# Second matmul of each attention score block: 64 rows of a head against 128 rows with zeros beside them

## The chip, the cores and the metric

The kernel runs on one core of one Trainium2 chip. The metric is the device time of one launch in microseconds (us); the number used is the median of the runs. A core has five engines with queues of their own: PE (TensorE, matmuls; PEld is its weight load, which can run beside a matmul), DVE (VectorE), ACT (ScalarE), POOL (GpSimd) and SP (SyncE, which here only issues transfers). Each engine takes its instructions in order and waits on semaphores for the others.

## What is computed

One decoder layer over 1024 prompt tokens and 32 sample tokens (8 sequences of 4): an mLSTM of 4 heads beside a dilated attention of 8 heads of 64, an output projection, a cross attention over a memory of 256, and a SwiGLU, all in float32. What the change touches is the attention over the prompt. The reference runs three dilated windows and weighs them by their softmax denominators:

```python
for window, d in DILATED:
    ...
    s = jnp.einsum('bdnqhe,bdnkhe->bdnhqk', qs, kb) * scale
    s = jnp.where(valid[None, :, None, :, :], s, -jnp.inf)
    p, lse = softmax_lse(s)
    ...
return combine_branches(outs, lses)
```

The kernel does the same as one causal softmax over all earlier keys, with the logarithm of how many windows hold a key added to its score (table LM). So each head needs, for each tile of 128 query tokens, the product of its q (64 channels) with its k (64 channels) over 128 to 1024 keys.

## The kernel before, in words

Float32 products run as fp32r, in parts: a value is split into a high part (rounded to fp32r) and a low part (the rest), and a product is made of high times high, high times low and low times high. In the big projections (`unit`, `tunit`) that is three matmuls of 128 rows for each slice of 128 channels.

The mixing layer goes over four pairs of heads (i = 0 to 3). For each: `project_qk(i)` makes q and k of the pair; `attention(i)` is a generator whose steps are traced as side work between the units of the projections that follow (`hook`): in pair 0 between the units of `project_m`, in pairs 1 to 3 between the token tiles of `project_v`. All matmuls are issued by one helper line, L276, and all transposes of the attention by L651.

`project_qk` lays a head's q out so that one matmul of 128 rows makes two of the three products: buffer `qz[hh]` holds the head's high part on one half of the partitions and its low part on the other half, `kz[hh]` holds the high part of k on both halves. The first matmul of a score block, `qz` times `kz`, is therefore (high + low) times high, over 128 rows. What is left is high times low: the low parts of k lie in `kl`, head 0 on partitions 0 to 63, head 1 on partitions 64 to 127, and the second matmul of the block takes the 64 partitions of its own head alone (`qz[hh][r, q]` times `kl[r, ks]`). Both add into the same PSUM bank.

A job is one query tile t (0 to 7) of one head hh; its 128(t+1) keys are done in one or two blocks (512 and the rest; 640 is 384 and 256). That is 12 blocks a head, 24 a pair, 96 in all. A step of the generator makes the scores of job j (PE), adds LM and takes the row maximum (DVE, L633), takes the exponential (ACT, L638), divides (DVE, L639 and L640); a few jobs later (`lag`: 2 in pairs 0 to 2, 1 in pair 3) `turn` transposes the probabilities (PE, L651) and copies them out of PSUM (L652, on ACT and DVE in turn), and `values` multiplies them with v into 64 columns each.

The order on PE, DVE, ACT and POOL is set by a scheduler from the traced order and its own cost estimates; the SP queue keeps the order in which it was written. Buffers are columns of a few big arenas: `f_all` and `f_x` for float32, `g_all` for high and low parts.

Of the kernel before, what the change touches and what calls it, by code (L numbers as in the profile page):

```python
# [31 lines left out]
# columns of the packed per-channel parameters  # L32
# [5 lines left out]
class Arena:  # L38
    """Columns of one memory location, taken and given back while the program is traced."""
# [41 lines left out]
class Zone:  # L81
    """Arenas that serve one kind of data."""
# [11 lines left out]
class Parts:  # L94
    """Tiles [P, n] as a high and a low part each, that the tensor engine multiplies at its full rate."""
# [39 lines left out]
def body(tc, ctx, I, O):  # L135
# [5 lines left out]
    # F: float32, G: high and low parts; NX and NY change over from one to the other.  # L141
# [9 lines left out]
    ar.arenas.append(arena(xpool.enter_context(tc.tile_pool(name="sbx", bufs=1)), NX + NY, "f_x"))  # L151
# [64 lines left out]
    # where the high and the low part of a slot are  # L216
# [3 lines left out]
    # the slot of a weight tile, and the tile whose readers have to be traced before it is loaded  # L220
# [28 lines left out]
    def weight():  # L249
        """The next weight tile: [P, 8, 128] as high and low parts."""  # L250
        j = W.at
        wload(j)
        W.at += 1
        return wtile(j)

    def weights(n):
        """The next n weight tiles, to be used together."""
        wload(W.at)
        out = [wtile(j) for j in range(W.at, W.at + n)]
        W.at += n  # L260
        assert W.at <= W.sent
        return out

    def weight_pair():
        """The next two weight tiles as one moving operand by k, [P, 2, 128], and their order."""
        wload(W.at)
        out = []
        for part in range(2):
            a, b = (wat[slot_of[j]][part] for j in (W.at, W.at + 1))
            lo, step = min(a, b), abs(a - b)  # L270
            out.append(R(gall[:, lo:lo + 2 * step]).rearrange("p (a x) -> p a x", a=2))
        W.at += 2
        return tuple((lambda k, v=v: v[:, :, P * k:P * k + P]) for v in out), a < b
# [6 lines left out]
    def later(units, fn):  # L280
        """Trace fn after that many more units of the tensor engine's work."""
        pending.append([units, fn])
# [15 lines left out]
    def hook(n=1):  # L298
        """Trace the next n pieces of the work that goes between units."""
        for _ in range(n):  # L300
            while sides:
                try:
                    next(sides[0])
                    break
                except StopIteration:
                    sides.pop(0)
# [5 lines left out]
    def unit(out, w, x, n0, n, K=KT):  # L312
        """out = sum over k of w[k].T x[k], from high and low parts."""
        s = slice(n0, n0 + n)
        for k in range(K):
            mm(out, w[0][:, k], x.rh(k, s), k == 0, False)
            mm(out, w[0][:, k], x.rl(k, s), False, False)
            mm(out, w[1][:, k], x.rh(k, s), False, k == K - 1)

    def tunit(out, x, n0, n, w, by_pass=False):  # L320
        """out = sum over k of x[k].T w[k]: tokens on partitions."""
        s = slice(n0, n0 + n)
        passes = [(x.rh, 0), (x.rh, 1), (x.rl, 0)]
        todo = [(k, p) for p in passes for k in range(KT)] if by_pass else [(k, p) for k in range(KT) for p in passes]
        for j, (k, (xp, a)) in enumerate(todo):
            mm(out, xp(k, s), w[a](k), j == 0, j == len(todo) - 1)

# [1 line left out]
    small = Ring([ar.take(12) for _ in range(12)])  # L329

    def newton(v, n):
        """v[:, :n] ** -0.5, by bits and three Newton steps."""
        h, y, a = small.next()[:, :n], small.next()[:, :n], small.next()[:, :n]
        vec.tensor_scalar(h, v, -0.5, None, ALU.mult)
        vec.tensor_scalar(y.bitcast(I32), v.bitcast(I32), -0.5, float(0x5F3759DF), ALU.mult, ALU.add)
        for _ in range(3):
            if n > 3:
                vec.tensor_tensor(a, y, y, ALU.mult)
                vec.tensor_tensor(a, a, h, ALU.mult)
                vec.scalar_tensor_tensor(y, a, 1.5, y, ALU.add, ALU.mult)  # L340
                continue
            c = [slice(j, j + 1) for j in range(n)]
            for j in c:
                vec.scalar_tensor_tensor(a[:, j], y[:, j], h[:, j], y[:, j], ALU.mult, ALU.mult)  # L344
            for j in c:
                vec.scalar_tensor_tensor(y[:, j], a[:, j], 1.5, y[:, j], ALU.add, ALU.mult)  # L346
        return y

    def rstd(sqs, n, rcol, rbc):
        """From squares [P, n], to be added up: 1/rms by token as columns, and over all partitions; two steps to trace."""  # L350
# [29 lines left out]
    ones = ar.take(P)  # L380
    vec.memset(ones.ap, 1.0)

# [10 lines left out]
    # buffers of the attention, and of the mLSTM; x, the sample's attention and the memory have them for a while  # L393
# [17 lines left out]
    def squares(raw, n):  # L411
        """The squares' sums over k, in place."""
# [54 lines left out]
    # buffers of an iteration  # L467
# [3 lines left out]
    # a head's q: high and low parts on a half of the partitions each; its k: high parts on both, low parts as q's high  # L471
    qz, kz = ([qkz[:, NP * (2 * a + hh):NP * (2 * a + hh) + NP] for hh in range(2)] for a in range(2))
    kl = qkz[:, 4 * NP:5 * NP]
    tmp = Ring([take(384) for _ in range(4)])
# [18 lines left out]
    # gates  # L493
    ig_tm = take(64)
    gr = take(2 * 160).view(k=2, t=160)
# [5 lines left out]
    def gates():  # L501
        ga = Arena(bcbuf.ap, bcbuf.n)
        ge = [ga.take(160) for _ in range(4)]
        pb = mb()
# [22 lines left out]
        # prompt: rows (chunk, head)  # L527
# [5 lines left out]
        vec.tensor_tensor_scan(b_, ones[:32, 0:128], lf[:, 0:128], 0.0, op0=ALU.mult, op1=ALU.add)  # L533
# [29 lines left out]
        # sample: rows head, columns (t, b)  # L563
# [27 lines left out]
        # to tokens on partitions, and over all partitions  # L591
# [11 lines left out]
        mm(p2[:, 192:224], ones[:32, :], wcd[:32, :], True, True)  # L603
# [9 lines left out]
    def attention(i):  # L613
        # the third buffer and the fourth are the mLSTM's, but the sample's attention has these in the last iteration
# [4 lines left out]
        sxs, pts = {}, {}  # L619

        def scores(j):
            t, hh = jobs[j]
            cn = P * (t + 1)
            r, q = slice(64 * hh, 64 * hh + 64), slice(P * t, P * t + P)
            sx = sxs[j] = SX.next()
            last = None
            for o, w in ((0, 384), (384, 256)) if cn == 640 else [(o, min(512, cn - o)) for o in range(0, cn, 512)]:
# [3 lines left out]
                mm(pb[:, :w], R(qz[hh][r, q]), R(kl[r, ks]), False, True)  # L631
# [31 lines left out]

        for j in range(15 + vlag):
            if j < 16:
                scores(j)
            if 0 <= j - lag < 16:
# [6 lines left out]
    def conv(j, n0, n, ps, dst):  # L674
        """Block n0..n0+n of tile j of the conv: its raw projection is ps times rstd."""
# [27 lines left out]
    def mlstm(h):  # L703
# [5 lines left out]
        # exp(u_s - mu_t), causal  # L709
# [23 lines left out]
        # the states between chunks, in place of what they come from  # L733
# [23 lines left out]
        # sample  # L757
# [30 lines left out]
        # divide, LayerNorm, gate  # L788
# [282 lines left out]
    qkz.drop()  # L1071
    for b in phase:
# [12 lines left out]
    def residual(xin, src, spill, xout, g, blocks):  # L1085
        """x = xin @ w + src, spilled; its parts times g, and the sums of its squares."""
# [36 lines left out]
    def xkv(j):  # L1123
        """A half of the memory's K or V."""
# [17 lines left out]
    def xscores(hp, t):  # L1142
        """The probabilities of two heads for 128 tokens."""
# [46 lines left out]
    def xsample():  # L1190
        """The sample's attention over the memory's caches, in pieces to trace between the others' work."""
# [68 lines left out]
    def xgroup(hp, n0, n):  # L1260
        """A pair of heads for a block, in pieces to trace between units."""
# [139 lines left out]
def layouts(x):  # L1401
    """The program's inputs: the arrays in the program's order of dimensions, and tables of shapes."""
# [4 lines left out]
    def chan(a):  # L1407
        """[n, 1024] to [128, 8, n]."""
        return c(a.T.reshape(8, P, -1).transpose(1, 0, 2))

    def wt(w):
        """[1024, N] to tiles [N / 128, 128, 8, 128]."""
# [30 lines left out]
    # tables  # L1443
# [21 lines left out]
def unpack(o):  # L1465
    """The reference's outputs from the program's."""
# [3 lines left out]
    def tok(a):  # L1470
        """[128, k, n] to [n, k * 128]."""
# [36 lines left out]
```

## Time and profile before

| | us |
|---|---|
| time, median of 3 runs (1815.0 to 1819.98) | 1817.07 |
| profiled execution: span from the first to the last instruction | 1815.7 |
| PE busy in that span | 1778.4 (98%) |
| PEld busy | 1678.2 (92%) |
| DVE busy | 989.5 (54%) |
| ACT busy | 568.0 (31%) |
| POOL busy | 256.8 (14%) |

The profile names the span alone as the profiled execution's own time. A PE that is shown busy is not a PE at its peak: a matmul's shown duration reaches from its start to its modelled end, and the next one starts before that end. What a matmul costs in a stream is the distance from its start to the next start. PEld's rows show the same from the other side: the time that the weight load stood idle before an instruction.

### The profile page before, as it was taken

The page shows a single profiled execution, that of the slowest core. Times are in us where ns is not written, and L with a number is a line of the kernel's source. Part 1 is how long each engine was busy: PE and PEld are TensorE (multiplying, and loading weights), DVE is VectorE, ACT ScalarE, POOL GpSimd, SP SyncE. Part 2 cuts the span into 40 slices and gives each one's busy share as a digit, 9 for nine tenths or more (in the row PEclk, how much of TensorE's full clock was granted, in tenths as well). Part 3 has the DMA queues.
Part 4 walks back from the last instruction along what each step waited for, and adds up shares of the span by engine and source line. Part 5 has one row for each costly group of instructions (what it writes and reads, how often), then busy time and mean ns, then how long its engine had stood idle before and what let it go on. Part 6 is the DMA issues. An engine that isn't in the chain of part 4 may idle for free.

```text
span 1815.7 us, 29027 instructions
## 1 busy us (share of the span) xinstructions
PE 1778.4 (98%) x11720; PEld 1678.2 (92%) x11720; DVE 989.5 (54%) x2418; ACT 568.0 (31%) x1132; POOL 256.8 (14%) x318
## 2 busy tenths in 40 slices
PE   6999999999999999999999999999999999999996
PEld 6879889889867899989989999999999999999996
DVE  7877676677646754666554535334433433444346
ACT  5344343343324453344343222211111120211214
POOL 3200200100100313200014211100101010010114
PEclk9999999999999999999999999999999999999998
DMA  4202112112233664475444511111111110111102
GB/s 164 67 31 74 56 53 73 52 55 71 96 111 135 205 217 142 143 254 199 151 148 141 192 51 47 48 36 58 47 35 47 47 59 24 59 47 47 47 13 96
DMA packets 60648, 165.09 MB, mean 91 GB/s; under 512 B 7234, under 2 KB 27618, under 8 KB 59874
## 3 DMA queue, kind: packets, MB, share of 16 engines
q1 hardware_dynamic: 52834, 139.79, 23.2%
q0 software_dynamic: 7680, 23.45, 3.6%
q8 instruction: 92, 1.51, 0.4%
q14 instruction: 42, 0.34, 0.1%
HBM read 135.41 MB, written 27.80 MB: 90 GB/s over the span
## 4 chain that ended last, share of the span: by engine, by line
PE 91%; DVE 5%; DMA 2%; ACT 1%; issue 1%; POOL 0%; DVEq 0%; SPq 0%; ACTq 0%; POOLq 0%
PE banks L276 88%; PE banks L651 2%; DVE g_all L409 1%; DVE g_all L235 1%; DVE f_all L1375 1%; DMA f_all<-in_w_mq_dram 1%; DMA f_x<-rowsD 1%; ACT g_all L234 0%; DVE f_x L693 0%; PE banks L1170 0%; DVE f_all L346 0%; DMA f_all<-in_xT_dram 0%; PE banks L818 0%; DMA f_all<-in_w_mk_dram 0%; DVE f_all L344 0%
## 5 line engine op out<-in xcount | busy, mean ns | idle before, releaser
L276 PE MATMUL banks<-g_all 128*128 128x384 f32 (+5 forms) x7104 | 1210.0, 321 | 12.7 <-DVE g_all L427 9.5
L276 PEld LDWEIGHTS banks<-g_all 128*128 128x128 f32 (+1 forms) x7104 | 1104.3, 189 | 63.5 <-issue 40.5
L276 PE MATMUL banks<-g_x,g_all 128*128 128x384 f32 (+3 forms) x1272 | 250.0, 325 | 0.0
L234 ACT CAST g_all<-f_all 128x1024 fp32r<-128x1024 f32 x136 | 141.6, 1047 | 277.2 <-PE banks L276 227.3
L276 PEld LDWEIGHTS banks<-g_x,g_all 128*128 128x128 f32 x1272 | 212.9, 189 | 0.7 <-issue 0.4
L235 DVE TENSOR_TENSOR g_all<-f_all,g_all 128x1024 fp32r<-128x1024 f32 x136 | 173.7, 1281 | 57.8 <-ACT g_all L234 57.4
L1355 DVE SCALAR_TENSOR_TENSOR f_all<-banks,f_all 128x384 f32<-128x384 f32 (+3 forms) x192 | 98.8, 522 | 133.1 <-PE banks L276 132.7
L1337 POOL TENSOR_TENSOR f_y<-f_y 128x384 f32<-128x384 f32 (+1 forms) x66 | 62.3, 943 | 637.8 <-DVE f_y L1336 637.8
L276 PE MATMUL banks<-g_all,g_x 128*128 128x384 f32 (+1 forms) x864 | 148.4, 323 | 0.0
L276 PEld LDWEIGHTS banks<-g_all,g_x 128*128 128x128 f32 x864 | 140.6, 188 | 0.0
L1336 DVE TENSOR_TENSOR f_y<-banks,f_all 128x384 f32<-128x384 f32 (+1 forms) x66 | 34.6, 524 | 109.2 <-PE banks L276 109.2
L276 PE MATMUL banks<-f_x 128*128 128x129 f32 (+6 forms) x542 | 84.7, 312 | 1.3 <-DVE f_x L724 0.9
L276 PEld LDWEIGHTS banks<-f_x 128*128 128x128 f32 (+3 forms) x542 | 60.8, 166 | 14.1 <-issue 4.7
L1333 DVE TENSOR_TENSOR f_y<-banks,f_all 128x384 f32<-128x384 f32 (+1 forms) x66 | 34.6, 524 | 68.7 <-PE banks L276 67.4
L1334 ACT ACTIVATE f_y<-f_y 128x384 f32<-128x384 f32 (+1 forms) x66 | 32.8, 497 | 124.4 <-DVE f_y L1333 124.4
L1095 DVE TENSOR_TENSOR f_all<-banks,f_all 128x384 f32<-128x384 f32 (+1 forms) x48 | 25.1, 522 | 73.8 <-PE banks L276 73.8
L276 PE MATMUL banks<-g_x 128*128 128x384 f32 (+3 forms) x288 | 63.1, 327 | 0.0
L1339 ACT CAST g_x<-f_y 128x384 fp32r<-128x384 f32 (+1 forms) x36 | 17.5, 487 | 117.5 <-POOL f_y L1337 117.5
L1335 DVE SCALAR_TENSOR_TENSOR f_y<-f_y 128x384 f32<-128x384 f32 (+1 forms) x66 | 34.5, 523 | 28.5 <-ACT f_y L1334 28.5
L276 PE MATMUL banks<-f_all,f_x 128*64 128x128 f32 (+4 forms) x558 | 48.8, 276 | 0.9 <-DVE f_x L537 0.9
L276 PEld LDWEIGHTS banks<-g_x 128*128 128x128 f32 x288 | 49.3, 191 | 0.1
L276 PEld LDWEIGHTS banks<-f_all,f_x 128*64 128x64 f32 (+4 forms) x558 | 37.4, 133 | 12.4 <-issue 7.2
(326 smaller groups left out, 1552.0 us busy)
## 6 DMA issues: line engine op xcount, KB each, us to landing
f_all<-in_w_mq_dram SPq DMA_DIRECT2D x24, 512.0 KB, 4.5
f_all<-in_w_gate_dram SPq DMA_DIRECT2D x22, 512.0 KB, 3.3
f_all<-in_w_up_dram SPq DMA_DIRECT2D x22, 512.0 KB, 3.3
f_all<-in_w_down_dram SPq DMA_DIRECT2D x22, 512.0 KB, 3.3
f_all<-in_w_cm_dram SPq DMA_DIRECT2D x20, 512.0 KB, 3.6
f_all<-in_memK_dram SPq DMA_DIRECT2D x16, 512.0 KB, 5.9
f_all<-in_memV_dram SPq DMA_DIRECT2D x16, 512.0 KB, 3.5
f_all<-x3T SPq DMA_DIRECT2D x4, 1056.0 KB, 4.9
```

Source lines behind the costliest of these rows:

```text
L234: act.copy(R(dst_hi), raw)
L235: eng.tensor_tensor(R(dst_lo), raw, dst_hi, ALU.subtract)
L276: pe.matmul(out, l, r, start=start, stop=stop)
L409: vec.scalar_tensor_tensor(x.rl(k, o), raw[:, k], col(g + k), x.hi(k, o), ALU.mult, ALU.subtract)
L651: pe.transpose(pb[:, c:c + P], sx[:, o + c:o + c + P], ident.ap)
L1095: vec.tensor_tensor(x, pb[:, :n], t, ALU.add)
L1333: vec.tensor_tensor(z, pg[:, :n], rbc[:, n0:n0 + n], ALU.mult)
L1334: act.activation(th, z, AF.Tanh, scale=0.5)
L1335: vec.scalar_tensor_tensor(z, th, 1.0, z, ALU.add, ALU.mult)
L1336: vec.tensor_tensor(bu, pu[:, :n], rbc[:, n0:n0 + n], ALU.mult)
L1337: gp.tensor_tensor(z, z, bu, ALU.mult)
L1355: vec.scalar_tensor_tensor(x, pb[:, :n], 0.5, x, ALU.mult, ALU.add)
```

## The change

The second matmul of a score block gets a stationary operand of 128 rows: the head's high part of q on its own 64 partitions, zeros on the other 64. It multiplies the low parts of k of both heads (`kl` on all 128 partitions); the zeros take the other head's away. The high part is copied by ACT into one of two buffers of 128 columns for each head (`pad`), two jobs ahead; a buffer comes up again four jobs later. The zeros are written once, at the start, by DVE. Room for the four buffers comes from a new small arena (`g_p`, 384 columns, taken from the end of `f_x`) and 128 columns of `g_all`; to make up for it a tile of ones is dropped (`one[:, 0:1]`, broadcast, stands for it) and the gates' staging tile `gr` moves into a buffer that the mLSTM uses later. The rest of the diff takes comments out.

```diff
-    ar.arenas.append(arena(xpool.enter_context(tc.tile_pool(name="sbx", bufs=1)), NX + NY, "f_x"))
+    ar.arenas.append(arena(xpool.enter_context(tc.tile_pool(name="sbx", bufs=1)), NX + NY - 3 * P, "f_x"))
+    padz = arena(xpool.enter_context(tc.tile_pool(name="sbq", bufs=1)), 3 * P, "g_p")
...
-    ones = ar.take(P)
-    vec.memset(ones.ap, 1.0)
...
+    qpad = [Ring([padz.take(P), padz.take(P) or gz.take(P)]) for _ in range(2)]
+    for ring in qpad:
+        for b in ring.items:
+            vec.tensor_scalar(R(b.ap), ident.ap, 0.0, None, ALU.mult)
...
-    gr = take(2 * 160).view(k=2, t=160)
...
+        gr = ga.take(2 * 160).view(k=2, t=160)
...
+        def pad(j):
+            t, hh = jobs[j]
+            r = slice(64 * hh, 64 * hh + 64)
+            qps[j] = qpad[hh].next()
+            act.copy(R(qps[j][r]), qz[hh][r, P * t:P * t + P])
...
-            r, q = slice(64 * hh, 64 * hh + 64), slice(P * t, P * t + P)
+            q, qp_ = slice(P * t, P * t + P), qps.pop(j)
...
-                mm(pb[:, :w], R(qz[hh][r, q]), R(kl[r, ks]), False, True)
+                mm(pb[:, :w], R(qp_.ap), R(kl[:, ks]), False, True)
...
+        pad(0), pad(1)
         for j in range(15 + vlag):
             if j < 16:
                 scores(j)
+            if j < 14:
+                pad(j + 2)
```

On PE the order stays. This is pair 1, query tiles 2 and 3, before; a row gives the shape that is written, so the second matmul of a block reads like the first (the "x2" of 384 and of 512 columns are one block each):

```order
179 L276 MATMUL banks<-g_all 128x384 x2
180 L651 MATMUL banks<-f_all,f_x 128x128 x2
181 L276 MATMUL banks<-g_all 128x384 x2
182 L651 MATMUL banks<-f_all 128x128 x2
183 L276 MATMUL banks<-f_all,f_x 64x128 x2
184 L276 MATMUL banks<-g_all 128x256 x24
185 L276 MATMUL banks<-g_all 128x512 x2
186 L651 MATMUL banks<-f_all 128x128 x3
```

The same place of the changed kernel (L660 is the transpose, L277 the helper, `g_p` the new buffers):

```order
207 L277 MATMUL banks<-g_all 128x384
208 L277 MATMUL banks<-g_all,g_p 128x384
209 L660 MATMUL banks<-f_all,f_x 128x128 x2
210 L277 MATMUL banks<-g_all 128x384
211 L277 MATMUL banks<-g_all,g_p 128x384
212 L660 MATMUL banks<-f_all 128x128 x2
213 L277 MATMUL banks<-f_all,f_x 64x128 x2
214 L277 MATMUL banks<-g_all 128x256 x24
215 L277 MATMUL banks<-g_all 128x512
216 L277 MATMUL banks<-g_all,g_p 128x512
217 L660 MATMUL banks<-f_all 128x128 x3
```

Every matmul stands where it stood; only the second of each block has another stationary operand.

On ACT there are 64 new copies. This is the start of pair 1's attention before (L865 takes v out of PSUM, L638 is the exponential, L652 the copy of transposed probabilities):

```order
114 L865 ACTIVATE f_x<-banks,f_all 128x128 x2
115 L638 ACTIVATE f_all,f_x<-f_all,f_x 128x128 x2
116 L865 ACTIVATE f_x<-banks,f_all 128x128
117 L652 COPY f_all<-banks 128x128
118 L638 ACTIVATE f_x<-f_x 128x256
119 L638 ACTIVATE f_all,f_x<-f_all,f_x 128x256
120 L865 ACTIVATE f_x<-banks,f_all 128x128
```

And of the changed kernel (L628 is the new copy, L877, L647 and L661 are what L865, L638 and L652 were):

```order
128 L877 ACTIVATE f_x<-banks,f_all 128x128 x2
129 L628 CAST g_p<-g_all 64x128 x2
130 L647 ACTIVATE f_all,f_x<-f_all,f_x 128x128 x2
131 L877 ACTIVATE f_x<-banks,f_all 128x128
132 L628 CAST g_p<-g_all 64x128
133 L628 CAST g_all<-g_all 64x128
134 L661 COPY f_all<-banks 128x128
135 L647 ACTIVATE f_x,f_all<-f_x,f_all 128x256
136 L647 ACTIVATE f_all<-f_all 128x256
137 L877 ACTIVATE f_x<-banks,f_all 128x128
```

The copies for jobs 0 to 3 stand further ahead, among the casts of `project_qk`; those shown are for jobs 4 to 7, each pair of them ahead of the exponentials or of the copy that stood there.

On DVE, at the start, before (L427 and L428 are the parts of the first v weights, L409 the low parts of x):

```order
8 L427 CAST g_all<-f_all 128x1056
9 L409 SCALAR_TENSOR_TENSOR g_all<-f_all,g_all 128x128
10 L428 TENSOR_TENSOR g_all<-f_all,g_all 128x1056
11 L427 CAST g_all<-f_all 128x1056
12 L409 SCALAR_TENSOR_TENSOR g_all<-f_all,g_all 128x128
13 L428 TENSOR_TENSOR g_all<-f_all,g_all 128x1056
14 L409 SCALAR_TENSOR_TENSOR g_all<-f_all,g_all 128x128
```

And of the changed kernel (L476 writes the zeros; L425, L426 and L407 are what L427, L428 and L409 were):

```order
9 L425 CAST g_all<-f_all 128x1056
10 L476 TENSOR_SCALAR g_p<-f_all 128x128
11 L426 TENSOR_TENSOR g_all<-f_all,g_all 128x1056
12 L476 TENSOR_SCALAR g_p<-f_all 128x128 x2
13 L476 TENSOR_SCALAR g_all<-f_all 128x128
14 L407 SCALAR_TENSOR_TENSOR g_all<-f_all,g_all 128x128 x2
15 L407 SCALAR_TENSOR_TENSOR g_all<-f_x,f_all,g_all 128x256 x8
```

Four new instructions stand ahead of the last low parts of the first chunk of x and of all of the second chunk's. The SP queue is unchanged.

## Rows read from the trace of the kernel before

**Rows 1.** The page: busy time, granted clock in 40 slices, chain by engine.

```profile
PE 1778.4 (98%) x11720; PEld 1678.2 (92%) x11720; DVE 989.5 (54%) x2418; ACT 568.0 (31%) x1132; POOL 256.8 (14%) x318
...
PEclk9999999999999999999999999999999999999998
...
PE 91%; DVE 5%; DMA 2%; ACT 1%; issue 1%; POOL 0%; DVEq 0%; SPq 0%; ACTq 0%; POOLq 0%
```

**Rows 2.** Stages with attention: start:end, length, busy time by engine, granted clock.

```profile
84.00:96.00 12.00, 12.00 (x40) 9.98 (x40) 6.18 (x24) 3.64 (x9) 0.00 (x0) 0.57 0.44 158
96.00:136.00 40.00, 40.00 (x237) 29.07 (x236) 30.70 (x105) 18.11 (x43) 2.70 (x5) 1.00 0.03 9
...
198.00:250.00 52.00, 52.00 (x378) 40.86 (x376) 32.05 (x115) 22.10 (x55) 5.22 (x9) 1.00 0.10 31
...
467.00:522.00 55.00, 55.00 (x408) 43.07 (x407) 33.09 (x118) 21.67 (x57) 6.46 (x12) 1.00 0.22 77
```

**Rows 3.** Timeline of PEld, two blocks of 512: start, duration, [idle before].

```profile
122.19 0.19 PEld L276 LDWEIGHTS banks<-g_all 128*128 128x128 f32 x1 [0.17 <-issue]
122.62 0.18 PEld L276 LDWEIGHTS banks<-g_all 64*128 64x128 f32 x1 [0.25 <-issue]
123.05 0.19 PEld L276 LDWEIGHTS banks<-g_all 128*128 128x128 f32 x1 [0.25 <-issue]
123.48 0.18 PEld L276 LDWEIGHTS banks<-g_all 64*128 64x128 f32 x1 [0.25 <-issue]
123.91 0.32 PEld L651 LDWEIGHTS banks<-f_all 128*128 128x128 f32 x3 [0.24 <-DVE f_x L637]
```

**Rows 4.** Timeline of PEld, blocks of 384 and projection matmuls of 384.

```profile
96.37 0.18 PEld L276 LDWEIGHTS banks<-g_all 64*128 64x128 f32 x1 [0.19 <-issue]
96.73 0.19 PEld L276 LDWEIGHTS banks<-g_all 128*128 128x128 f32 x1 [0.18 <-DVE f_x L633]
97.11 0.18 PEld L276 LDWEIGHTS banks<-g_all 64*128 64x128 f32 x1 [0.19 <-issue]
```

**Rows 5.** Timeline of PE, output projection: 384 columns, 128 rows, no attention.

```profile
1010.13 1.39 PE L276 MATMUL banks<-g_all 128*128 128x384 f32 x7
1011.36 0.34 PE L276 MATMUL banks<-g_x,g_all 128*128 128x384 f32 x1
1011.53 0.34 PE L276 MATMUL banks<-g_all 128*128 128x384 f32 x1
```

**Rows 6.** Weight loads of 64 rows, all: busy, mean ns, idle before.

```profile
L276 PEld LDWEIGHTS banks<-g_all 64*128 64x128 f32 x96 | 17.8, 187 | 18.6 <-issue 15.3
```

**Rows 7.** Timeline of PEld where two loads of 64 rows are neighbours.

```profile
107.92 0.19 PEld L276 LDWEIGHTS banks<-g_all 64*128 64x128 f32 x2 [0.19 <-issue]
108.29 0.47 PEld L276 LDWEIGHTS banks<-g_all 128*128 128x128 f32 x3 [0.19 <-issue]
```

**Rows 8.** ACT copies near the new one in size, by line and shape.

```profile
L661 ACT COPY f_x<-banks 128x128 f32<-128x128 f32 x19 | 5.0, 262 | 15.5 <-PE banks L276 11.3 <-issue 4.1
L843 ACT CAST g_all<-f_x 64x256 fp32r<-64x256 f32 x14 | 5.7, 405 | 2.9 <-DVE f_x L838 2.7
```

**Rows 9.** Timelines of DVE and PE: L640 divides, L651 then transposes; pairs 1 and 3.

```profile
202.33 0.29 DVE L640 TENSOR_SCALAR f_all<-f_all,f_x 128x128 f32<-128x128 f32 x1
...
204.53 0.33 PE L651 MATMUL banks<-f_all 128*128 128x128 f32 x1
...
487.77 0.49 DVE L640 TENSOR_SCALAR f_all<-f_all,f_x 128x512 f32<-128x512 f32 x1
...
488.33 0.64 PE L651 MATMUL banks<-f_all 128*128 128x128 f32 x4
```

**Rows 10.** Timeline of DVE at the start: low parts of x's second chunk.

```profile
13.76 4.68 DVE L409 SCALAR_TENSOR_TENSOR g_all<-f_x,f_all,g_all 128x256 fp32r<-128x256 f32 x8 [1.52 <-ACT g_all L408]
```

**Rows 11.** Waits of PEld, 198 to 250 us: total us, times, longest.

```profile
PEld banks L276 <- issue: 7.0, 34, 0.2
...
PEld banks L651 <- DVE f_x L633: 0.4, 2, 0.2
```

More of the change, by code (lines that the diff above doesn't have):

```diff
@@ L532, in gates @@
         b_, m_ = u1[:, 0:128], c[:, 0:128]
-        vec.tensor_tensor_scan(b_, ones[:32, 0:128], lf[:, 0:128], 0.0, op0=ALU.mult, op1=ALU.add)
+        vec.tensor_tensor_scan(b_, one[:32, 0:1].to_broadcast([32, P]), lf[:, 0:128], 0.0, op0=ALU.mult, op1=ALU.add)
         u_ = stk[:32, :]
@@ L602, in gates @@
         vec.tensor_scalar(wcd[:32, :], ident[:32, :32], t2[:32, 4:5], None, ALU.mult)
-        mm(p2[:, 192:224], ones[:32, :], wcd[:32, :], True, True)
+        mm(p2[:, 192:224], one[:32, 0:1].to_broadcast([32, P]), wcd[:32, :], True, True)
         vec.tensor_copy(wcb.ap, p2[:, 192:224])
@@ L618, in attention @@
         jobs = [(t, hh) for t in range(8) for hh in range(2)]
-        sxs, pts = {}, {}
+        sxs, pts, qps = {}, {}, {}
+        def pad(j):
[3 more added lines that the diff above has]
+            act.copy(R(qps[j][r]), qz[hh][r, P * t:P * t + P])
         def scores(j):
@@ L1071, in body @@
     qkz.drop()
+    qpad[1].items[1].drop()
     for b in phase:
```

## Prediction

> **What bounds the kernel now.** I read the page first, for who is busy and what the chain that ended last is made of, then the stages with attention, then single steps of PE there. On the page PE is busy 98% of a span of 1815.7 us and makes up 91% of the chain; no other engine passes 54% [rows 1]. So PE's stream is the bound, and a change is worth what it takes out of that stream or adds to it. But busy is not at its peak: in the stages with attention PE shows 100% as elsewhere, while its weight loads are busy only 29.07 of 40 us, 40.86 of 52 and 43.07 of 55 [rows 2]. Something lies between the loads there. The waits say that it is no other engine: from 198 to 250 us the loads stood idle 34 times for 7.0 us with nothing to wait for ("issue"), and what is put down to DVE is 0.4 us, in pieces of the same 0.2 us [rows 11].
>
> The timeline of the loads shows where. In two blocks of 512 columns a load starts every 0.43 us, with 0.25 us idle before it, at each change from a load of 128 rows to one of 64 and at each change back [rows 3]. In blocks of 384 the steps are 0.36 and 0.38 us, with 0.18 to 0.19 idle [rows 4]. The same 384 columns at 128 rows cost 1.23 / 7 = 0.176 us a step in a projection, with the same parts of high and low adding into one bank, so neither the size nor the adding is to blame [rows 5]. A change of the row count thus costs 0.37 - 0.176 = 0.19 us at 384 columns. For 512 the streaming is 0.176 x 512 / 384 = 0.235, and 0.43 - 0.235 = 0.195: the same price whatever the length. Over all 96 loads of 64 rows the idle time before them is 18.6 us, 0.194 each [rows 6], which is the change into them alone.
>
> **The change part by part.**
>
> *PE, removed.* 96 matmuls of 64 rows become 96 of 128, in the same places. Their columns don't change and a load of 64 rows takes 0.18 us against 0.19 for one of 128 [rows 3], so the matmul itself costs the same. What goes is 192 changes of the row count: 192 x 0.19 = 36.5 us.
>
> Two corrections. In five blocks the next matmul is one of `values`, which writes 64 columns and keeps a stall of its own; I leave 0.1 us in each, 0.5 us. And in one place two matmuls of 64 rows, one of each head, stand side by side: both loads fit in 0.19 us [rows 7], so there is no change between them (2 x 0.19 less to gain) and they ran beside each other, which is lost (0.12 us for 256 columns by the step of 384). That is 0.5 us. Left: 35.5 us.
>
> This one place is where a rule of the Trainium skill speaks against the change: TensorE: Matmul & The Clock Gate, section Part 3: Packing small matmuls, says that matmuls on different row groups of the array run at the same time, starting some 4 ns apart. The trace agrees (two loads in 0.19 us), and by that rule the 64-row form could be the cheaper one if heads were paired. The order of before pairs them once in 96, so by the rule the change loses what is counted above and no more.
>
> *ACT, added.* 64 copies of 64 x 128. The trace has none of that shape: a copy of 128 x 128 takes 262 ns and a cast of 64 x 256 takes 405 [rows 8]. The bounds are 0.2 and 0.4 us; I take 0.28, near the first, whose columns it has. 16 x 0.28 = 4.5 us a pair of heads, 18 us in all, beside ACT's 22.10 of 52 us [rows 2]. With PE 9 us shorter the stage has 43 us and ACT 26.6 (62%), DVE 32.05 (75%). That cover holds on average. Queued behind a copy on ACT are exponentials and the copies out of PSUM, for which DVE and PE wait. But a copy's buffer was read by the job four earlier, and the copy is due two jobs later, so it rarely waits itself. Cost zero in pairs 1 and 2. Were the cover gone, 18 us would come back.
>
> *What is late next.* Where PE gets shorter, turns come sooner after their scores, and the row chain DVE, ACT, DVE in between does not shrink. In pair 1 the first division ends at 202.62 and its transpose starts at 204.53, 1.91 us later [rows 9]; that is the smallest of that pair's 16 distances, the others go up to 6.7. Between a job's scores and its turn the stream loses one change out and one or two jobs with two changes a block: 0.19 + 2 x 0.38 = 0.95 us while a job is one block, twice that when it is two and the distance is over 3. Nothing is lost in pairs 1 and 2. In pair 3 (lag 1) the division of job 6 ends at 488.26 and PE starts the transpose at 488.33 [rows 9]; jobs 0 and 2 are as tight, the rest have 0.8 us and more. There PE already waits as soon as it comes earlier: between scores and turn 0.19 + 0.38 = 0.57 us goes for a one-block job, so about 0.5 us is given back three times, and 0.1 to 0.2 in the four with 0.8 to 0.95 us, where two-block jobs lose 0.95. That is 2.0 us. Pair 0's distances lie between those of pairs 1 and 3; I take 0.5 us. ACT's new copies ahead of pair 3's tight exponentials add up to 0.28 us each; 0.5 us. Sum given back: 3.0 us; bounds 0 and 12 (as if half of the gain of pair 3, 4.5 us, and of pair 0, 4.5 us, and 3 us of copies came back).
>
> *The start.* Four writes of zeros on DVE, 128 x 128, at about 0.29 us as L640 takes [rows 9]: 1.2 us. They end before the low parts of x's second chunk, for which DVE stood idle 1.52 us waiting for ACT [rows 10]; that idle time hides them. Uncovered they would cost 1.2 us. The dropped ones, the moved `gr` and the broadcast `one` take away or move instructions of a tenth of a microsecond on DVE; zero, bounds 0.5 either way.
>
> *The clock.* From 84 to 96 us the granted clock is 0.57, mostly the lower of its two levels, 1.2 against 2.4 GHz; in the other stages with attention it is 1.00 [rows 2]. Four blocks fall into that stretch. If denser work ends it sooner, or another stall in the start moves it, up to 12 x (1 - 0.57) = 5 us are at stake. I take zero, and 2.5 either way for the range.
>
> *Sum.* 35.5 - 3.0 = 32.5 us less. Against the profiled execution: 1815.7 - 32.5 = 1783.2 us of span. That execution's span is 1.4 us under the median of the runs shown, so the median would be 1817.1 - 32.5 = 1784.6; I say 1785 us. The likeliest case's own range: 1776 (nothing given back, the clock helps: 38 us less, and 3 us for a price of 0.205 at each change) to 1794.
>
> **The rivals.**
>
> *The stall is not from the row count.* It could belong to reading q's columns as a new stationary operand, or to the second product closing the bank. Then 128 rows stall as well, and nothing is gained: 1817 plus 0 to 3 us. For it: the 64-row load is always the block's second and last. Against it: the projections change their stationary operand and close banks in the same way without a gap [rows 5], and the stall is there on the way out too [rows 3]. The Trainium skill, TensorEngine Tiling (Array Packing), Key Properties, says that a change of the tiling mode drains the engine; no price stands there, and the rows above give it. 5%.
>
> *Half comes back as waits.* The row chain or ACT becomes the bound in the stages with attention: DVE's 75% leaves little for its bursts (L633 and L640 of two heads, and copies), PSUM banks come free later than PE wants them. For it: by the trace's reading PE's transposes wait for L633 already now and then [rows 11], and pair 3 is tight. Against: the distances of pairs 1 and 2. It would give 12 to 20 us back: about 1800 us. 13%.
>
> *Slower: the new copies block ACT.* If a copy stands in ACT's queue until PE has read its buffer, every exponential and every copy out of PSUM behind it stands too, v's from `project_v` among them, and PE waits for their banks. It decides from 35.5 / 64 = 0.55 us of PE's time per copy on; at 0.75 us each, a copy with a wait on the other engine's end, the kernel ends at 1817 + 12 = 1829. For it: PE's wait on ACT is new in each job, and the order sets copies ahead of exponentials. Against: two buffers a head, so the copy's wait was over before. 4%.
>
> *More than the sum.* Also the row after a block streams sooner, or the clock recovers early: below 1776. 5%.
>
> **How the numbers follow.** Likeliest 73%, half back 13%, no effect 5%, slower 4%, more than the sum 5%. A measurement of this kernel tells 0.3% (5.5 us) from no change. Faster takes the likeliest, half back and more than the sum: 0.91. No effect lies within 0.3%: 0.05. Slower: 0.04. The range of 8 in 10 reaches from 1776 to 1800: it takes in the likeliest and half of the case in which half comes back, and the bounds of what is given back (12 us) and of the clock.
>
> **What would show it.** Right: the loads of 64 rows are gone; steps in a block of 512 columns fall from 0.43 to about 0.235 us, with under 0.05 us idle before each; PEld is busy some 41 of the 43 us that pair 1's stage then takes; the stages shrink by 8 to 9.5 us each, the rest of the kernel stays. Wrong: steps of 0.43 us at 128 rows (the stall is another's); idle time of PE put down to L628's successors or to DVE and ACT lines, in pairs 1 and 2 above all (waits took the gain's place); a start that is longer than 84 us before the first block; a stretch at the lower clock within the attention.

## The result, and the profile after

The changed kernel takes 1783.78 us (median of 4 runs, 1782.08 to 1785.85) against 1816.03 us of the kernel before on the same chip (4 runs, 1811.72 to 1819.98): ratio 0.983, 95% interval 0.981 to 0.985. It is 32 us faster; forecast were 1785 us and 32.5 us less. The profiled execution has a span of 1780.3 us, 35.4 less than that of before.

The page of the changed kernel first: busy time by engine, then the chain by engine.

```profile
PE 1742.5 (98%) x11720; PEld 1671.6 (94%) x11720; DVE 987.0 (55%) x2421; ACT 585.2 (33%) x1196; POOL 258.2 (15%) x318
...
PE 88%; DVE 6%; DMA 3%; ACT 1%; issue 1%; POOL 0%; SPq 0%; DVEq 0%; ACTq 0%; POOLq 0%
```

Against [rows 1], PE's busy time falls by 35.9 us at the same count of instructions, and that of its weight loads by only 6.6: what went is time between the loads. ACT gains 64 instructions and 17.2 us. PE is still busy 98% of the span and makes up 88% of the chain (91% before); the bound has not moved to another engine.

The stage table of the changed kernel (start:end, length, busy time by engine, granted clock):

```profile
84.00:96.00 12.00, 12.00 (x69) 11.06 (x68) 10.32 (x41) 7.68 (x24) 0.41 (x1) 0.86 0.40 144
96.00:136.00 40.00, 40.00 (x331) 35.20 (x331) 36.71 (x117) 24.41 (x56) 3.70 (x7) 1.00 0.04 13
198.00:250.00 52.00, 52.00 (x427) 47.79 (x427) 38.09 (x111) 26.55 (x59) 5.01 (x8) 1.00 0.16 51
```

PE is shown 100% busy here as it was in [rows 2]. The difference is in the counts and the loads: from 198 to 250 us 427 matmuls where there were 378, and the loads busy 47.79 of 52 us where it was 40.86. (The windows are the same times, not the same work; the loads' share is what compares.) The 378 matmuls that took PE from 198 to 250 us before, pair 1's attention and the projection around it, now take this stretch:

```profile
186.23:230.20 43.97, 43.97 (x378) 40.00 (x376) 30.41 (x112) 25.36 (x67) 5.22 (x9) 1.00 0.11 38
```

That is 44.0 us instead of 52, with the loads busy 40.0 of it.

Step by step, the loads of two 512-column blocks of the changed kernel (timeline of PEld: start, duration):

```profile
224.92 0.19 PEld L277 LDWEIGHTS banks<-g_all,g_p 128*128 128x128 f32 x1
225.15 0.19 PEld L277 LDWEIGHTS banks<-g_all 128*128 128x128 f32 x1
225.38 0.19 PEld L277 LDWEIGHTS banks<-g_all,g_p 128*128 128x128 f32 x1
225.61 0.92 PEld L660 LDWEIGHTS banks<-f_all 128*128 128x128 f32 x7
```

The steps are 0.23 us and no idle time is shown before a load, where [rows 3] have 0.43 with 0.25 idle. That is the 0.235 us foretold. The group of loads of the new operand as far as it lies in `g_p` (72 of the 96; busy us, mean ns, idle before):

```profile
L277 PEld LDWEIGHTS banks<-g_all,g_p 128*128 128x128 f32 x72 | 14.0, 195 | 0.6
```

The waits of PEld from 198 to 250 us (total us, times, longest):

```profile
PEld banks L277 <- issue: 2.1, 12, 0.2
PEld banks L660 <- DVE f_x L642: 0.3, 1, 0.3
```

The loads have 0.6 us of idle time before 72 of them, against 18.6 before 96 in [rows 6]; and 2.1 us of "issue" where [rows 11] have 7.0.

Where along the program it came: but for four matmuls at the start that swap places (35 to 40 us before), every PE instruction stands at the same place in both orders, so the same one can be looked up in both. These are the first transposes of the probabilities in pairs 1, 2 and 3, in the changed kernel (timeline of PE):

```profile
191.92 0.27 PE L660 MATMUL banks<-f_all 128*128 128x128 f32 x1
...
317.88 0.27 PE L660 MATMUL banks<-f_all 128*128 128x128 f32 x1
...
443.29 0.33 PE L660 MATMUL banks<-f_all 128*128 128x128 f32 x1 [0.38 <-DVE f_all L649]
```

In the kernel before, the first of them started at 204.53 [rows 9], the others here:

```profile
338.84 0.33 PE L651 MATMUL banks<-f_all 128*128 128x128 f32 x1
...
471.53 0.31 PE L651 MATMUL banks<-f_all 128*128 128x128 f32 x1
```

They come earlier by 12.61, 20.96 and 28.24 us. By the same comparison over all of PE's instructions, the lead is 0.8 us when the attention begins, grows by 11.0 in pair 0, 8.1 in pair 1, 8.1 in pair 2 and 6.5 in pair 3 to 34.7, and stays between 34.7 and 36.1 for the rest of the kernel. Between pairs 1 and 2 it grows by 0.3 us at a single place (298 us before), where PE waits less for DVE. Apart from this and the 0.8 us of the start, the gain lies in the four stretches with score blocks.

### The profile page after: what moved, and what is told of

It reads as the page before. It is cut to its first block, busy times and chain, and to the rows that moved or that the text cites. A ratio compares the mean times of both kernels' runs of the same rounds, so it can differ in the third digit from the quotient of the medians.

```text
span 1780.3 us, 29119 instructions
## 1 busy us (share of the span) xinstructions
PE 1742.5 (98%) x11720; PEld 1671.6 (94%) x11720; DVE 987.0 (55%) x2421; ACT 585.2 (33%) x1196; POOL 258.2 (15%) x318
## 4 chain that ended last, share of the span: by engine, by line
PE 88%; DVE 6%; DMA 3%; ACT 1%; issue 1%; POOL 0%; SPq 0%; DVEq 0%; ACTq 0%; POOLq 0%
PE banks L277 85%; PE banks L660 2%; DMA f_x<-rowsD 1%; DVE g_all L407 1%; DVE g_all L236 1%; DVE f_all L1388 1%; ACT g_all L235 1%; DMA f_all<-in_w_mq_dram 1%; DMA f_all<-mixT 1%; DVE f_x L705 0%; PE banks L1183 0%; DMA f_all<-in_w_mv_dram 0%; DMA f_all<-in_xT_dram 0%; DMA f_all<-in_w_mk_dram 0%; PE banks L830 0%
## 5 line engine op out<-in xcount | busy, mean ns | idle before, releaser
L277 PE MATMUL banks<-g_all 128*128 128x384 f32 (+5 forms) x7032 | 1172.3, 319 | 11.4 <-DVE g_all L425 8.6
L277 PEld LDWEIGHTS banks<-g_all 128*128 128x128 f32 (+1 forms) x7032 | 1087.5, 189 | 35.8 <-issue 16.9
L277 PE MATMUL banks<-g_x,g_all 128*128 128x384 f32 (+3 forms) x1272 | 250.2, 325 | 0.0
L277 PEld LDWEIGHTS banks<-g_x,g_all 128*128 128x128 f32 x1272 | 213.0, 189 | 0.7 <-issue 0.4
L277 PE MATMUL banks<-g_all,g_x 128*128 128x384 f32 (+1 forms) x864 | 148.4, 323 | 0.0
L277 PEld LDWEIGHTS banks<-g_all,g_x 128*128 128x128 f32 x864 | 140.6, 188 | 0.0
L277 PE MATMUL banks<-f_x 128*128 128x129 f32 (+8 forms) x606 | 91.3, 306 | 1.1 <-DVE f_x L736 0.6
L277 PEld LDWEIGHTS banks<-f_x 128*128 128x128 f32 (+4 forms) x606 | 66.9, 158 | 14.7 <-issue 5.7
L277 PE MATMUL banks<-g_x 128*128 128x384 f32 (+3 forms) x288 | 63.1, 327 | 0.0
L277 PE MATMUL banks<-f_all 128*32 128x256 f32 (+4 forms) x376 | 39.1, 353 | 11.4 <-DVE f_all L347 6.0
L277 PE MATMUL banks<-f_all,f_x 128*64 128x128 f32 (+4 forms) x558 | 49.3, 276 | 0.8 <-DVE f_x L540 0.8
L277 PEld LDWEIGHTS banks<-f_all,f_x 128*64 128x64 f32 (+4 forms) x558 | 37.7, 133 | 12.9 <-issue 5.5
```

The costliest lines, as they stand in the source:

```text
L277: pe.matmul(out, l, r, start=start, stop=stop)
```

## The experiments

Edits are shown against the changed kernel. Runs of one group shared a chip and its runs of the kernel before.

**Row count or anything else of the change?** Two kernels take the change apart: one has all of its copies, buffers and zeros but multiplies the 64 rows alone; the other multiplies 128 rows without any copy, by taking `qz` itself, both parts of q, as the operand.

```diff
-                mm(pb[:, :w], R(qp_.ap), R(kl[:, ks]), False, True)
+                r = slice(64 * hh, 64 * hh + 64)
+                mm(pb[:, :w], R(qp_[r]), R(kl[r, ks]), False, True)
```

> The changed kernel with all copies and zeros kept, but the second matmul again of 64 rows: it takes the head's half of the copied buffer. If the gain is the row count alone (each change of the row count costs PE 0.19 us), all 192 changes are back and the time is that of the kernel before, 1816 us, plus what the copies cost, 0 to 3 us: 1814 to 1820. If the gain came from a fresh stationary buffer instead of columns of q (rival), the time stays near 1784. If it came from the clock at the start, which the copies' place may have shifted, the time lies some 5 us under the kernel before.

Measured: 1814.12 us (10 runs, 1811.26 to 1819.01), before 1815.22; ratio 0.9998 (0.9985 to 1.0012). Its loads of 64 rows from `g_p`:

```profile
L277 PEld LDWEIGHTS banks<-g_all,g_p 64*128 64x128 f32 x72 | 13.3, 187 | 13.4 <-issue 10.4 <-ACT g_p L628 0.4 <-ACT f_x L704 0.3
```

The same operand in the same buffers, read over 64 rows, has 13.4 us idle before 72 loads; over 128 rows it had 0.6. All the rest of the change together is worth nothing that can be measured, either way.

```diff
-            act.copy(R(qps[j][r]), qz[hh][r, P * t:P * t + P])
...
-                mm(pb[:, :w], R(qp_.ap), R(kl[:, ks]), False, True)
+                mm(pb[:, :w], R(qz[hh][:, q]), R(kl[:, ks]), False, True)
```

(Here the other 64 rows hold the head's low part of q instead of zeros, so a product that the reference doesn't have is added.)

> The second matmul of 128 rows straight from q's buffer with high and low parts, and no copies: it adds the other head's product with the low part, so the scores are off; it leaves out the 64 copies and every wait for them. If row count is all, the 192 changes are gone as in the changed kernel, and what it is faster by is what the copies and the waits for them cost: 0 to 3 us, 1781 to 1784. If the copies cost much (ACT's 18 us or waits of PE in each job), it is 8 us faster or more, 1776 or less. If a buffer of its own for the stationary operand is what counts, it is back at 1816.

Measured: 1780.91 us (1777.62 to 1783.14), ratio 0.9811 (0.9792 to 0.9831). 128 rows alone give the whole gain; the 64 copies cost nothing that the time shows.

**The price of one visit to 64 rows.** The second matmul is cut into 64 columns and the rest. In one kernel the 64 columns are multiplied over 64 rows, in the other over 128; both have 96 matmuls more.

```diff
-                mm(pb[:, :w], R(qp_.ap), R(kl[:, ks]), False, True)
+                r = slice(64 * hh, 64 * hh + 64)
+                mm(pb[:, :64], R(qp_[r]), R(kl[r, o:o + 64]), False, False)
+                mm(pb[:, 64:w], R(qp_.ap), R(kl[:, o + 64:o + w]), False, True)
```

> The changed kernel with the second matmul of each block cut in two: its first 64 columns by 64 rows, the rest by 128. That puts one 64-row matmul, with a change in and a change out, back into each of the 96 blocks, over a small part of the columns. By a price for each change of 0.19 us it costs 192 x 0.19 = 36 us over the same cut with 128 rows in both parts: about 1822 if that one is at 1787. If the price went with the columns that run at 64 rows (a slower matmul), 64 of some 350 columns would cost about a fifth, 7 us: about 1794.

```diff
-                mm(pb[:, :w], R(qp_.ap), R(kl[:, ks]), False, True)
+                mm(pb[:, :64], R(qp_.ap), R(kl[:, o:o + 64]), False, False)
+                mm(pb[:, 64:w], R(qp_.ap), R(kl[:, o + 64:o + w]), False, True)
```

> The same cut in two with 128 rows in both parts: one matmul and one weight load more a block, no change of the row count. By the price of a change: 1784 plus 96 short matmuls at 0.03 to 0.06 us, 1787 to 1790. If another stationary operand or closing the bank costs 0.19 us or more (rival), 96 to 192 of these are added: 1802 to 1820.

Measured: with 64 rows 1821.86 us (1819.17 to 1823.07; ratio 1.0039, 1.0028 to 1.0049), with 128 rows 1792.11 us (1790.23 to 1794.67; 0.9875, 0.9857 to 0.9893). The difference is 29.8 us over 96 visits to 64 rows, 0.31 us each; the prediction's 0.38 would have made 36. The mean granted clocks of the two are 0.991 and 0.993, so a part of it can be the clock; in pairs 1 and 2, at 2.4 GHz in both profiles, PE's stream differs by 7.1 us for 24 visits, 0.30 each. The kernel with 128 rows itself lies above the 1787 to 1790 expected for it (see the last section). Timelines of PE for the end of a 384-column block and the whole 256-column block behind it, 64 rows first:

```profile
217.98 0.64 PE L277 MATMUL banks<-g_all,g_p 64*128 64x64 f32 x2
218.46 0.28 PE L277 MATMUL banks<-g_all 128*128 128x256 f32 x1
218.67 0.58 PE L277 MATMUL banks<-g_all,g_p 64*128 64x64 f32 x2
219.08 0.38 PE L662 MATMUL banks<-f_all 128*128 128x128 f32 x2
```

and with 128 rows in their place:

```profile
207.38 0.42 PE L277 MATMUL banks<-g_all,g_p 128*128 128x64 f32 x2
207.63 0.28 PE L277 MATMUL banks<-g_all 128*128 128x256 f32 x1
207.75 0.37 PE L277 MATMUL banks<-g_all,g_p 128*128 128x64 f32 x2
207.96 0.60 PE L661 MATMUL banks<-f_all 128*128 128x128 f32 x4
```

"x2" is the short matmul and the rest behind it. From the first matmul of the 256 block to the short one are 0.21 us against 0.12, 0.09 more. From the short one to the transposes are 0.41 against 0.21, 0.20 more. Over the 89 visits at 2.4 GHz the means are 0.09 more for the step into the short matmul, 0.19 for its own step and 0.02 for the step behind it. The short matmul stands alone between two changes, so its step can hold a part of both; these are not the prices of the way in and the way out. The first of the orders below, which puts two 64-row matmuls in a row, takes them further apart.

**Half of the visits.** Head 0 with 128 rows, head 1 with 64: 48 visits.

```diff
-                mm(pb[:, :w], R(qp_.ap), R(kl[:, ks]), False, True)
+                r = slice(64 * hh, 64 * hh + 64)
+                if hh:
+                    mm(pb[:, :w], R(qz[hh][r, q]), R(kl[r, ks]), False, True)
+                else:
+                    mm(pb[:, :w], R(qp_.ap), R(kl[:, ks]), False, True)
```

> Half of the change: the second matmul has 128 rows for head 0 of each pair and 64 rows, as before, for head 1; all copies kept. 48 visits to 64 rows are left of 95. By a price for each visit (a change in and one out, 0.31 us by the last two runs, 0.34 by the pairs of the changed kernel) it lies 15 to 16 us over the changed kernel: 1797 to 1800. If the gain is bound by something else that full speed hits (waits that take part of it), more than half is there already: 1790 or less.

Measured: 1798.66 us (1795.41 to 1799.64), before 1813.49; ratio 0.9911 (0.9891 to 0.993). 14.8 us for 48 matmuls, 0.31 each: the gain goes with the count of visits.

**64 rows with fewer visits.** Instead of widening the matmuls, their order can be changed. In the first kernel a job of two blocks makes both first matmuls, then both second ones (74 groups of 64-row matmuls where before had 95); in the second both heads of a query tile go together, their turns too, in twos (62 groups; 34 of them hold two matmuls, one of each head, side by side); the third has that same order with 128 rows. The two with 64 rows have no copies.

```diff
...
-                mm(pb[:, :w], R(qz[hh][:, q]), R(kz[hh][:, ks]), True, False)
-                mm(pb[:, :w], R(qp_.ap), R(kl[:, ks]), False, True)
...
+            for pb, (o, w) in zip(pbs, cuts):
+                mm(pb[:, :w], R(qz[hh][:, q]), R(kz[hh][:, o:o + w]), True, False)
+            for pb, (o, w) in zip(pbs, cuts):
+                mm(pb[:, :w], R(qz[hh][r, q]), R(kl[r, o:o + w]), False, True)
...
```

> 64 rows as before, no copies, but in jobs of two blocks both first matmuls come before both second ones. The 96 matmuls of 64 rows then stand in 74 groups instead of 95, 22 of them of two that use the same rows. If what costs is the change of the row count, 21 visits less at 0.31 to 0.34 us: 6.5 to 7 us under the kernel before, about 1808. If each matmul of 64 rows has its price, the time stays at 1815.

```diff
...
+                for hh in range(2):
+                    mm(pbs[hh][:, :w], R(qz[hh][:, q]), R(kz[hh][:, o:o + w]), True, False)
+                for hh in range(2):
+                    r = slice(64 * hh, 64 * hh + 64)
+                    mm(pbs[hh][:, :w], R(qz[hh][r, q]), R(kl[r, o:o + w]), False, True)
...
```

> 64 rows, no copies, both heads of a query tile done together: first matmuls of both, then second matmuls of both, on different halves of the partitions. 34 of 48 pairs stand side by side, 62 groups. 33 visits less at 0.31 to 0.34 us are 10 to 11 us, and if neighbours on different rows run at the same time, as the one pair in the kernel before did, 34 x 0.2 us more: 1797 to 1800, against 1804 if they run one after the other. Turns come in twos too, which the next run tells apart.

```diff
...
+                for hh in range(2):
+                    mm(pbs[hh][:, :w], R(qps[j + hh].ap), R(kl[:, o:o + w]), False, True)
...
```

> The same order of heads with 128 rows and copies as in the changed kernel. No change of the row count: 1784 as the changed kernel, and what it is off from that is the price of the order alone. By the price of a visit the 64-row run lies 62 x 0.32 - 34 x 0.2 = 13 us over this one.

Measured, with before at 1813.49: 1805.54 us (1804.14 to 1806.91; ratio 0.9952, 0.9934 to 0.997), 1796.54 us (1791.95 to 1800.31; 0.9901, 0.9877 to 0.9925) and 1781.93 us (1781.7 to 1782.36; 0.9822, 0.9802 to 0.9842). Fewer visits help without a single wider matmul: 8.0 us for 21 groups less, 0.38 each (0.26 to 0.57 by the interval). In the trace pairs 1, 2 and 3 gain 2.7 us each over the kernel before, for 7 groups less.

The first of these kernels also shows how a visit is made up. Timeline of PE for a job whose two 64-row matmuls stand in a row:

```profile
217.76 0.28 PE L277 MATMUL banks<-g_all 128*128 128x256 f32 x1
217.97 0.44 PE L277 MATMUL banks<-g_all 64*128 64x384 f32 x1
218.25 0.28 PE L277 MATMUL banks<-g_all 64*128 64x256 f32 x1
218.46 0.66 PE L662 MATMUL banks<-f_all 128*128 128x128 f32 x4
```

The step into the first is 0.21 us, where 256 columns take 0.12 in the changed kernel; the first's own step is 0.28, where 384 take 0.18; the second's is 0.21 against 0.12. The 21 such groups agree: 0.09 us more ahead of the visit, 0.10 to 0.11 in the first 64-row step, 0.09 in the second, and 0.06 in the first transpose behind it (0.17 against 0.11). That is 0.34 us for two matmuls. A visit of one, in the kernel before, costs as much: 0.09 ahead of it, 0.19 in its own step, 0.06 behind. So what costs is the visit and not each matmul of 64 rows. It reads as if each change lengthened the step ahead of it and the step behind it by some 0.1 us; a group of three, whose middle step would have no change beside it, was not run.

With the heads side by side 17 us are gained, but 128 rows in the same order are another 14.6 us faster. Some of the 14.6 is the clock: it was at its lower level for 6.8 us more near 84 us and for 3.4 us more near 618 us in the profile with 64 rows. Without that the two profiles differ by some 11 us over the score blocks. An estimate by prices comes out higher: 62 visits at 0.34 are 21 us, less what the 34 pairs gain by running beside each other, 34 x 0.176 us (the step of 384 columns, the mean block) = 6: 15 us. Where the rest stays was not looked into.

**Again, and the copies on another engine.**

> The changed kernel as it is, for a comparison on the same chip with the next two: 0.983 of the kernel before, 1782 to 1785.

```diff
-            act.copy(R(qps[j][r]), qz[hh][r, P * t:P * t + P])
+            gp.tensor_copy(R(qps[j][r]), qz[hh][r, P * t:P * t + P])
```

> The changed kernel with the 64 copies on POOL instead of ACT, where nothing of the attention's row chain stands behind them. The run without copies lay 0 to 5 us under the changed kernel. If the copies delay ACT's exponentials, it is 1 to 3 us faster than the changed kernel; if POOL takes them late and PE waits for them, 1 to 5 us slower; if they are hidden either way, the same within 1 us.

> 128 rows with both heads of a query tile together, once more, beside the changed kernel on the same chip: 1.5 to 2 us faster by the earlier runs' medians, if that was more than the difference between chips.

Measured, with before at 1813.1 (9 runs): the changed kernel 1781.09 us (1776.71 to 1782.91; ratio 0.9822, 0.9809 to 0.9835), copies on POOL 1781.92 (0.9832, 0.9818 to 0.9845), heads together with 128 rows 1783.87 (0.9839, 0.9825 to 0.9852). The three can't be told apart, and the 1.5 to 2 us expected of the last are not seen; no version with the same products beats the changed kernel.

## Why the prediction was right, point by point

**The bound and the stall.** Right. PE's stream was the bound, and what it lost was the change between 128 and 64 rows. The rival that the stall has another cause fell with the first two experiments: the same operand and the same closing matmul stall with 64 rows and don't with 128. The Trainium skill (TensorEngine Tiling (Array Packing), Key Properties) says that a change of tiling mode drains the engine; the traces agree, at 0.30 to 0.34 us for a visit there and back.

**192 x 0.19 = 36.5 us.** The mechanism was right, this term too large. Pairs 1 and 2, to which neither of the two corrections applies, gained 8.1 us each for 24 blocks, 0.34 a block instead of 0.38; over 96 blocks that is 32.4 us. A second profile of the changed kernel has the same 8.1 in both pairs. The error is the sentence "the same price whatever the length": it was read off steps of 384 and 512 columns, most with a change at either end. Compared matmul by matmul with the changed kernel, in the stretches at 2.4 GHz, such a step is indeed 0.19 us longer before, at 128 columns 0.14: that of a 64-row matmul (79 of 92 at 0.18 to 0.21), and that of a 128-row matmul between two visits (the first matmul of 30 of the 92 blocks). But 61 first matmuls have no visit ahead of them, and their steps are 0.08 to 0.10 longer; and a transpose behind a visit, of 128 columns, is only 0.05 to 0.06 longer. In pair 1 that makes 3.1 us ahead of the 64-row matmuls, 4.4 in their own steps and 0.6 elsewhere.

**Taken off: 1.0 us of corrections, 3.0 us given back.** Right in place, too much in size. Against 8.1 us in pairs 1 and 2, pair 3 gained 6.5 and pair 0, with 3.4 us of its 11.0 put down to the clock (below), 7.6: 1.6 and 0.5 us less, where 3.0 (2.0, 0.5 for copies, 0.5 ahead of `values`) and 1.0 (0.5 and 0.5 for the two matmuls side by side) were taken. In pair 3 the transposes now wait for the division, as foretold for job 6. The division on DVE's timeline of the changed kernel:

```profile
458.64 0.49 DVE L649 TENSOR_SCALAR f_all<-f_all 128x512 f32<-128x512 f32 x1
```

and its transposes on PE's:

```profile
459.18 0.66 PE L660 MATMUL banks<-f_all 128*128 128x128 f32 x4
```

The division ends at 459.13, PE starts 0.05 us later; jobs 0, 2 and 10 are as tight. In pair 1 the first division ends at 190.86,

```profile
190.57 0.29 DVE L649 TENSOR_SCALAR f_all<-f_all,f_x 128x128 f32<-128x128 f32 x1
```

and its transpose starts at 191.92: 1.06 us where it was 1.91. The stream loses 0.85 us in between (0.95 was worked out), and no distance of that pair falls below 1.0. So nothing was given back there, as foretold.

**The copies.** ACT's line of the changed kernel, for the 48 of 64 that go to `g_p`:

```profile
L628 ACT CAST g_p<-g_all 64x128 fp32r<-64x128 f32 x48 | 14.2, 296 | 6.7 <-PE banks L277 5.5
```

296 ns against the 280 taken. Their cover held nearly everywhere: by time the kernel without them and the one with them on POOL can't be told from the changed one. From 84 to 530 us the loads are put down as waiting 0.8 us in three places for L628, 0.6 of it in two places of pair 3 (at 450.4 and 456.2 us; the second profile has the same two). The kernel without copies gains 6.8 us in pair 3 and the one with them on POOL 6.9, against 6.5: that is 0.3 to 0.4 us for the copies, where 0.5 was set aside. The two rivals that rested on ACT and on waits, "half comes back" and "slower", are out by this and by the time.

**The start.** The zeros take 222 ns each (290 taken) and are hidden: the low parts of x's second chunk begin at 12.63 us where they began at 13.76 [rows 10], and PE is 0.8 us ahead when the attention begins.

**The clock.** Zero was taken, and for the timed runs that holds; in the profiled pair it does not. In the profile of before the granted clock was at its lower level, 1.2 GHz, for 10.2 us from 84.2 us on; in that of the changed kernel for 3.4 us from 84.3. From 75 to 84 us, ahead of the fall, PE had been busy 7.64 us in the first and 8.33 in the second, and in both the clock was back at 2.4 GHz after a stretch in which PE was shown busy throughout. Later, at 606.4 us before and 572.4 after, there is another such stretch, 6.8 and 3.4 us long; from 600 to 606 us and from 566 to 572 us, ahead of it, PE was busy 3.48 and 2.74 us. At half speed, 6.8 and 3.4 us less of it are worth 3.4 and up to 1.7 us (1.4 seen at the second). So some 4.8 of the 35.4 us between the two profiled spans are the clock. But the stretch at 84 us isn't a property of the kernel: in the second profile of the changed kernel it is 6.8 us long. Here is the stage table of the kernel with copies and 64 rows:

```profile
84.00:96.00 12.00, 12.00 (x45) 9.49 (x43) 7.52 (x29) 4.62 (x14) 0.00 (x0) 0.72 0.45 158
```

It takes as long as the kernel before, and has 0.72 here where that one had 0.57 [rows 2]. Over the timed runs with a clock on record, on several chips, the mean clock of the kernel before is 0.992 (33 runs, mean time 1813.9 us) and that of the changed one 0.992 too (8 runs, 1782.2 us): 31.7 us between them at an equal clock. By place the profiled pair gives 35.4 - 4.8 = 30.6; the 1.1 us between the two is less than single runs scatter.

**The sum.** 32.5 us forecast, 32 measured, comes out closer than its terms, which is in part luck: 4.1 too much for the changes, 1.9 too much taken off and 0.3 not foreseen (the wait at 298 us) leave 30.6, which is what the profiled pair shows without the clock.

## What to carry to other kernels

In a stream of 128-row matmuls a visit to 64 rows cost here, beside its columns, 0.30 to 0.34 us there and back, more than the 0.23 us of streaming 512 columns. Filling the rows with zeros cost PE nothing that the steps show (0.23 us for 512 columns), so it was the better form while the copy that lays out the operand was hidden; a cheaper half measure is an order with fewer visits (8 and 17 us of the 32). Such a loss hides behind an engine that is shown 100% busy: look at the steps between starts and at the load's idle time with no releaser, and price it by a pair of kernels that differ in the row count alone: the idle time of 0.19 us at each change, taken twice, gave 0.38 a block where 0.34 was measured.

## What the runs showed of the hardware

- A visit to 64 rows lengthens the step ahead of it by 0.09 us, that of a lone 64-row matmul by 0.19 (two in a row: 0.10 and 0.09) and that of a transpose behind it by 0.06. A lone 128-row matmul between two visits is 0.19 longer as well.
- Two 64-row matmuls on different halves, side by side, start within 0.003 to 0.004 us of each other in all 34 pairs and run beside each other, as the Trainium skill says (TensorE: Matmul & The Clock Gate, Part 3: Packing small matmuls). Still, with 34 such pairs in 62 visits the kernel was 14.6 us slower than with 128 rows, some 11 of it not the clock.
- Cutting a matmul in two is not free though no column is added: with 64 columns cut off, at 128 rows in both parts, the kernel took 1792.11 us against some 1783 (0.9822 x 1815.22), about 0.1 us for each of the 96. In the trace the short matmul's step is 0.03 us, its share of 0.23 for 512 columns; it is the matmul behind it that takes longer, 0.28 to 0.29 us for 448 columns, whose share would be 0.20.
- Matmuls that write 64 columns (`values`) still have idle time of 0.17 us before the next load, as in the first of [rows 3]. Whether this has the same cause, by columns instead of rows, was not tried.
